# Which engine waits for the last store of a two-tensor interleave: SyncE or GpSimd

## The chip, the cores and the metric

The kernel runs on one core of one Trainium2 chip. The metric is the time of one execution in microseconds on the device, for which the median of several runs is given. The profile is that of one execution; its span goes from the start of the first instruction of the kernel to the end of the last, so the time of the same execution is a little longer than its span.

## The reference

Two tensors x and y of 32 x 256 x 1024 float32 values (33.55 MB each) are interleaved along the last dimension. Nothing is calculated; every value is copied once.

```python
result = np.zeros((batch, seq, dim * 2), dtype=np.float32)
result[..., 0::2] = x
result[..., 1::2] = y
```

## The kernel before

Both inputs are cut into n = 8 pieces of 128 partitions x 8192 values (4 MB each), and piece k of the output is 128 x 16384 values. As each partition takes a contiguous run of the flat tensor, weaving x and y element by element in a partition gives the wanted output.

On chip there are two buffers for x, two for y (128 x 8192 values each, used in turn by k), and two output buffers ot0 and ot1, each of which holds half of an output piece (4 MB). The engines work side by side, each along its own queue, with semaphores between them:

- **SyncE** issues the loads. The first half of the first x piece is issued at L37 (ScalarE issues the other half at L38), and these two are moved by hand ahead of the opening barrier of the program. The loop at L40 issues x (L45) and y (L48) of every piece; from k = 2 on it first waits until VectorE has read the buffer (semaphore `woven`, L43 and L47).
- **VectorE** does the weaving. For each half h of a piece it copies x into the even columns of `ot[h]` (L60) and y into the odd ones (L63). It waits for the loads, and at L59 for the store that last emptied `ot[h]` (semaphore `osem[h]`).
- **ScalarE** issues the stores (L68), one of 4 MB for each half, when `woven` says that both copies are done. Store h adds 16 to `osem[h]` when it has landed.
- **GpSimd** and **TensorE** have no work in the body. GpSimd has four small memsets and its share of the barriers in the opening (L84 and L122 are lines of the set-up around the body).

Every DMA adds 1 to its semaphore from each of the 16 DMA engines. After the last store the semaphores have to be brought back to zero and the stores have to be waited for. ScalarE waits at L72 for the last but one store (`osem[0]` at 16 n = 128) and clears all semaphores but `osem[1]` in one instruction (L75). The very last store counts on `osem[1]`. SyncE waits for it at L76, with a no-operation that starts when `osem[1]` has reached 128 and then takes 128 from it, which brings it to zero. In the profile this instruction is an `EVENT_SEMAPHORE` of the engine's queue. Nothing follows it on SyncE.

Of the kernel before, what the change touches and what calls it, by code (L numbers as in the profile page):

```python
# [3 lines left out]


def _interleave(nc, x, y, out):
    P = 128
    W = 8192
    H = W // 2  # L10

    total = 1
    for s in x.shape:
        total *= s
    n = total // (P * W)
    assert n * P * W == total

    def rows(ap, names, k):
        flat = ap.rearrange("b s d -> (b s d)")
        return flat[k * names : (k + 1) * names].rearrange("(p w) -> p w", p=P)  # L20

    fp32 = mybir.dt.float32
    xt = [nc.alloc_sbuf_tensor(f"xt{b}", [P, W], fp32).ap() for b in (0, 1)]
    yt = [nc.alloc_sbuf_tensor(f"yt{b}", [P, W], fp32).ap() for b in (0, 1)]
    ot = [nc.alloc_sbuf_tensor(f"ot{b}", [P, W], fp32).ap() for b in (0, 1)]

    xsem = [nc.alloc_semaphore(f"xsem{b}") for b in (0, 1)]
    hsem = nc.alloc_semaphore("hsem")
    ysem = [nc.alloc_semaphore(f"ysem{b}") for b in (0, 1)]
    woven = nc.alloc_semaphore("woven")  # L30
    osem = [nc.alloc_semaphore(f"osem{b}") for b in (0, 1)]

    xs = [rows(x, P * W, k) for k in range(n)]
    ys = [rows(y, P * W, k) for k in range(n)]
    os_ = [rows(out, 2 * P * W, k) for k in range(n)]

    nc.sync.dma_start(out=xt[0][:, :H], in_=xs[0][:, :H]).then_inc(xsem[0], 16)  # L37
    nc.scalar.dma_start(out=xt[0][:, H:], in_=xs[0][:, H:]).then_inc(hsem, 16)  # L38

    for k in range(n):  # L40
        b = k % 2
        if k >= 2:
            nc.sync.wait_ge(woven, 4 * (k - 2) + 3)  # L43
        if k:
            nc.sync.dma_start(out=xt[b], in_=xs[k]).then_inc(xsem[b], 16)  # L45
        if k >= 2:
            nc.sync.wait_ge(woven, 4 * (k - 2) + 4)  # L47
        nc.sync.dma_start(out=yt[b], in_=ys[k]).then_inc(ysem[b], 16)  # L48

    for k in range(n):  # L50
        b = k % 2
        for h in (0, 1):
            c = slice(h * H, (h + 1) * H)
            if h == 0:
                nc.vector.wait_ge(xsem[b], 16 * (k // 2 + 1))
            elif k == 0:
                nc.vector.wait_ge(hsem, 16)
            if k:
                nc.vector.wait_ge(osem[h], 16 * k)  # L59
            nc.vector.tensor_copy(out=ot[h][:, 0::2], in_=xt[b][:, c]).then_inc(woven, 1)  # L60
            if h == 0:
                nc.vector.wait_ge(ysem[b], 16 * (k // 2 + 1))
            nc.vector.tensor_copy(out=ot[h][:, 1::2], in_=yt[b][:, c]).then_inc(woven, 1)  # L63

    for k in range(n):
        for h in (0, 1):
            nc.scalar.wait_ge(woven, 4 * k + 2 * h + 2)
            nc.scalar.dma_start(  # L68
                out=os_[k][:, h * W : (h + 1) * W], in_=ot[h]
            ).then_inc(osem[h], 16)  # L70

    nc.scalar.wait_ge(osem[0], 16 * n)  # L72
    used = sorted(s.num for s in [*xsem, hsem, *ysem, woven, osem[0]])
    assert used == list(range(used[0], used[-1] + 1)), used
    nc.scalar.sem_clear(range(used[0], used[-1] + 1))  # L75
    nc.sync.nop(nofuse=True).wait_op(osem[1], 16 * n, "sem-ge").then_inc(  # L76
        osem[1], -16 * n
    )


def kernel(tc, x, y, out):
    nc = tc.nc
    tc.close()
    tc.compile()  # L84

    _interleave(nc, x, y, out)

    blocks = nc.main_func.blocks
    for engine in (mybir.EngineType.SP, mybir.EngineType.Activation):
        opening = blocks[0].instructions  # L90
        at, moved = next(
            (b, i)
            for b in blocks[1:]
            for i in b.instructions
            if i.engine == engine and i.opcode == "DMACopy"
        )
        assert not (moved.sync_info and moved.sync_info.on_wait)
        body = at.instructions
        body.remove(moved)
        gate = next(  # L100
            n
            for n, i in enumerate(opening)
            if i.engine == engine and i.opcode == "Drain"
        )
        opening.insert(gate, moved)
        at.instructions = body
        blocks[0].instructions = opening


# [1 line left out]
_INS = ['x', 'y']  # L111
_OUTS = [((32, 256, 2048), 'float32')]


# [23 lines left out]
```

## Time and profile before

| what | value |
|---|---|
| runs before | 314.41, 314.45, 314.48, 314.58 us; median 314.47 |
| time of the profiled execution | 314.41 us |
| span of the profiled execution | 313.1 us (313.086) |
| instructions | 113 |
| data read and written | 67.11 MB and 67.11 MB, 429 GB/s over the span |
| VectorE busy | 72.6 us (23%), 32 copies |
| GpSimd busy | 0.2 us, 4 memsets, all in the first 0.5 us |
| last copy of VectorE ends | 298.2 us |
| last store issued | 298.24 us |
| ScalarE's clear (L75) starts | 303.40 us |
| SyncE's closing wait (L76) starts | 313.07 us |

In the profile's names, SP is SyncE, ACT is ScalarE, DVE is VectorE, POOL is GpSimd and PE is TensorE; a q behind the name means the queue of the engine, whose instructions (DMA issues, semaphore waits, drains) are not counted as busy time. Where a line gives three durations, these are the least, the median and the greatest in ns, followed by the first and last start in us. In the list of waits a line names who waited, for whom, the total in us, how often, and the longest. The trace also has a record of each update of a semaphore, with its time; those go on a little beyond the span.

### The profile page before, as it was taken

The page shows a single profiled execution, that of the slowest core. Times are in us where ns is not written, and L with a number is a line of the kernel's source. Part 1 is how long each engine was busy: PE and PEld are TensorE (multiplying, and loading weights), DVE is VectorE, ACT ScalarE, POOL GpSimd, SP SyncE. Part 2 cuts the span into 40 slices and gives each one's busy share as a digit, 9 for nine tenths or more (in the row PEclk, how much of TensorE's full clock was granted, in tenths as well). Part 3 has the DMA queues.
Part 4 walks back from the last instruction along what each step waited for, and adds up shares of the span by engine and source line. Part 5 has one row for each costly group of instructions (what it writes and reads, how often), then busy time and mean ns, then how long its engine had stood idle before and what let it go on. Part 6 is the DMA issues. An engine that isn't in the chain of part 4 may idle for free.

```text
span 313.1 us, 113 instructions
## 1 busy us (share of the span) xinstructions
DVE 72.6 (23%) x32; POOL 0.2 (0%) x4
## 2 busy tenths in 40 slices
DVE  0226002231022410324003250031501305013500
POOL 0000000000000000000000000000000000000000
DMA  8999999999999999999999999999999999999998
GB/s 341 463 406 398 465 406 456 414 452 419 435 435 419 452 402 469 402 469 402 465 406 461 410 452 419 435 435 427 444 406 465 402 469 402 465 406 461 410 456 347
DMA packets 4752, 134.22 MB, mean 429 GB/s; under 512 B 528, under 2 KB 528, under 8 KB 528
## 3 DMA queue, kind: packets, MB, share of 16 engines
q10 hardware_dynamic: 2448, 69.21, 51.2%
q1 hardware_dynamic: 2304, 65.01, 48.5%
HBM read 67.11 MB, written 67.11 MB: 429 GB/s over the span
## 4 chain that ended last, share of the span: by engine, by line
DMA 82%; DVE 12%; issue 0%
DMA out_dram<-ot 76%; DMA yt<-in_y_dram 6%; DVE ot L63 6%; DVE ot L60 6%
## 5 line engine op out<-in xcount | busy, mean ns | idle before, releaser
L60 DVE COPY ot<-xt 128x4096 f32<-128x4096 f32 x16 | 36.7, 2295 | 182.8 <-DMA out_dram<-ot 171.3
L63 DVE COPY ot<-yt 128x4096 f32<-128x4096 f32 x16 | 36.7, 2291 | 42.8 <-DMA yt<-in_y_dram 42.8
L122 POOL MEMSET const-bfloat16-1.0<- 128x1 bf16 x1 | 0.1, 102 | 0.0
L122 POOL MEMSET const-uint8-127<- 128x1 uint8 x1 | 0.1, 102 | 0.0
L122 POOL MEMSET const-float32-0.0<- 128x1 f32 x1 | 0.1, 99 | 0.2 <-issue 0.2
L122 POOL MEMSET const-float32-1.0<- 128x1 f32 x1 | 0.1, 99 | 0.0
## 6 DMA issues: line engine op xcount, KB each, us to landing
out_dram<-ot ACTq DMA_DIRECT2D x16, 4096.0 KB, 29.0
yt<-in_y_dram SPq DMA_DIRECT2D x8, 4096.0 KB, 60.8
xt<-in_x_dram SPq DMA_DIRECT2D x7, 4096.0 KB, 43.7
xt<-in_x_dram SPq DMA_DIRECT2D x1, 2048.0 KB, 11.6
xt<-in_x_dram ACTq DMA_DIRECT2D x1, 2048.0 KB, 13.2
```

The lines of the kernel that those rows point to most:

```text
L60: nc.vector.tensor_copy(out=ot[h][:, 0::2], in_=xt[b][:, c]).then_inc(woven, 1)
L63: nc.vector.tensor_copy(out=ot[h][:, 1::2], in_=yt[b][:, c]).then_inc(woven, 1)
L122: nc = _bacc.Bacc("TRN2", target_bir_lowering=False, num_devices=1)
```

## The change

The closing no-operation is issued on GpSimd's queue in place of SyncE's. Its wait (`osem[1]` at 16 n) and its update (minus 16 n) are the same. ScalarE's wait for the last but one store and its clear of the other semaphores stay as they are.

```diff
     nc.scalar.sem_clear(range(used[0], used[-1] + 1))
-    nc.sync.nop(nofuse=True).wait_op(osem[1], 16 * n, "sem-ge").then_inc(
+    nc.gpsimd.nop(nofuse=True).wait_op(osem[1], 16 * n, "sem-ge").then_inc(
         osem[1], -16 * n
     )
```

## Prediction

> **What bounds the kernel.** I read the chain of waits first. Nearly all of it is transfers: 82% of the chain is DMA, mostly stores, and VectorE has 12%. Its last pieces, the DMA issues and the queue waits are the part that the change touches.
>
> ```profile
> DMA 82%; DVE 12%; issue 0%
> ...
> out_dram<-ot ACTq DMA_DIRECT2D x16, 4096.0 KB, 29.0
> ```
>
> ```profile
> 265.56 28.13 DMA out_dram<-ot
> 293.69 0.02 issue
> 293.71 2.30 DVE ot L60
> 296.01 2.20 DVE ot L63
> ```
>
> The last copy ends at 298.21 us. ScalarE issues the last store at 298.24 and its 16 parts land from 312.66 to 313.05. Then only the end is left. For it I read the waits of SyncE's queue and the two closing lines, one by one:
>
> ```profile
> SPq L76 <- SPq L76: 85.9, 1, 85.9
> ```
>
> ```profile
> L76 SPq EVENT_SEMAPHORE  x1: 17/17/17, 313.1 to 313.1; - x1
> ```
>
> ```profile
> L75 ACTq EVENT_SEMAPHORE_RANGE_CLEAR  x1: 63/63/63, 303.4 to 303.4; - x1
> ```
>
> SyncE has sat at L76 since 227.2 us and starts it at 313.069, 16 ns after the last landing. ScalarE was through its own end at 303.467. The span stops when L76 ends (313.086 us), but the time of this execution is 314.41 us, so 1.32 us lie around the span. The semaphore updates of the trace show what comes behind it. Nothing in the kernel uses semaphore 2. It is updated in passes of nine, one pass just before the span, one broken into pieces in it and behind it, one at the very end. In us from the span's start:
>
> ```
> before:  -0.374 -0.340 -0.302 -0.258 -0.234 -0.123 -0.084 -0.050 -0.003
> middle:   1.794 303.585 303.624 303.668 313.220 313.264 313.303 313.337 313.384
> last:   314.170 314.204 314.243 314.286 314.309 314.409 314.447 314.481 314.528
> gaps, before: 34 38 44  24 111 39 34 47 ns (371 in all)
> gaps, middle:  - 39 44   - 44  39 34 47
> gaps, last:   34 39 43  23 100 38 34 47 (358 in all)
> ```
>
> I take this as a walk over the five engines, there and back: four steps out, a turning point, four steps home. The broken middle pass tells who is where. Its second update comes 118 ns after ScalarE's last instruction (303.467), its fifth 134 ns after SyncE's (313.086). So **ScalarE is second and SyncE is the turning point**. The first, at 1.794, belongs to an engine that was done early, which VectorE (busy until 298.2) was not. The length of the steps places the rest. At the barriers that open the kernel, all on one release, the wait instruction of each engine starts this long after the update:
>
> ```
> SyncE 16 ns, ScalarE 21, VectorE 28, TensorE 28 (releases at 0.825, 1.152, 1.480 us)
> GpSimd 24 ns, on its own semaphore (updates at 0.697, 1.025, 1.352 us)
> ```
>
> On the way home the steps are 44, 39, 34 and 47 ns. VectorE, GpSimd, ScalarE, TensorE would give this order (28, 24, 21 and 28, TensorE's instruction being the longest, 51 ns against 17 to 21). So **GpSimd is third and VectorE fourth**; I give that order 8 in 10. [...]
>
> **The change part by part.** One instruction moves from SyncE's queue to GpSimd's. No transfer, copy or semaphore value changes, and nothing else stood behind L76 in either queue.
>
> *Removed from SyncE.* Its 85.9 us of waiting cost nothing: after its last load was issued (226.830 to 227.158) it has nothing to do. It gets to its place in the walk early, but it cannot turn the walk before VectorE has passed it on. Worth 0 by itself.
>
> *Added to GpSimd.* It is idle from 1.5 us to the end, with no instruction of the kernel behind the wait, so nothing is held up inside the kernel. These rows show that the kind of instruction costs as much there as on SyncE:
>
> ```profile
> L84 POOLq EVENT_SEMAPHORE  x4: 17/17/17, 1.0 to 1.5; - x4
> ...
> L84 POOLq DRAIN  x2: 34/38/41, 0.9 to 1.2; - x2
> ...
> L84 SPq EVENT_SEMAPHORE  x2: 17/17/17, 1.2 to 1.5; - x2
> ```
>
> Duration: 17 against 17 ns, 0. Start after the last update: 24 against 16 ns, **+8 ns**. Way from its last instruction to its update of semaphore 2: the trace doesn't show it, as GpSimd was long there when ScalarE handed on. Bounds: ScalarE's 118 ns below, TensorE's 235 ns above if it is the first (1.559 to 1.794), against SyncE's 134: -16 to +101 ns. I take 134, **+0**, because GpSimd's and SyncE's steps elsewhere are alike (two neighbouring instructions 78 to 81 ns apart on GpSimd, 71 to 92 on SyncE). Were a drain in that way, it is 34 to 181 ns more (the longest is this one, with memsets before it):
>
> ```profile
> L122 POOLq DRAIN  x1: 181/181/181, 0.3 to 0.3; - x1
> ```
>
> *Moved: the place at which the walk is stopped.* Before, the late engine is the turning point: VectorE, GpSimd and ScalarE have gone out already (303.668 at the latest), and 44+39+34+47 = 164 ns of way home remain. After, the late one is third: outward to VectorE and SyncE is still to be done, and then home. What that takes is read from the whole passes, from the third update to the ninth: -0.302 to -0.003 = 299 ns, 314.243 to 314.528 = 285 ns. The middle pass had 164, so **+121 to +135 ns**. That is more than two steps (44+24 = 68): in whole passes the fourth engine needs 100 to 111 ns from the turn to its update, and 44 where it had waited long. I read this as its own time between two updates (135 and 123 ns); it would again have just updated. If that reading is wrong the sum is +68.
>
> [...]
>
> *Cover.* Neither ScalarE's end at L75 nor the copies move. SyncE's wait hid beside the transfer, GpSimd's does as well; only what follows the last landing counts, and nothing is beside that. [...]
>
> **Sum.** +8, +0, +128 (the middle of 121 and 135) = +136 ns. The profiled execution's 314.41 us becomes 314.55. The median of the runs is 0.06 above it, so 314.47 + 0.14 = **314.61 us**, +0.04%. Bounds: 8-16+68 = +60 ns below, 8+101+135 = +244 above, and 8+181+135 = +324 with the long drain, +425 with both. One case below that: if the time is not taken at the end of this sequence but where the kernel's last instruction ends, only +8 ns would be seen. Runs differ by 0.17 us among themselves (314.41 to 314.58).
>
> **The rivals.**
>
> *The walk is elsewhere, or isn't timed (no change, not slower).* If the clock that gives the time stops before the walk, the sum is +8 ns, 314.48 us. For it: I cannot see the stop. Against it: 1.32 us lie outside the span, and no transfer of the trace and no kernel instruction fills them. If GpSimd is first and not third, the whole pass counts, 358 to 371 less 164 = +194 to +207, 314.68 us; if fourth, 242 to 270 less 164 or so, +83 to +97, 314.57 us. Both are inside the forecast's own band.
>
> *GpSimd has more to do on its way out (slower, inside 0.2%).* A drain of 34 to 181 ns in its way, hidden so far behind ScalarE's 303.585: +0.17 to +0.32 us, 314.79 us at its long end.
>
> *GpSimd's next instructions are not at hand (slower for certain).* The mechanism on the other side of the bound: after 311 us at one instruction GpSimd has to fetch what follows, at the only place where nothing hides it. Price from this trace: instruction blocks of 8192 B take 0.31 to 0.49 us in transfer (11 to 8 us before the span), and the first transfer of the kernel starts moving 0.985 us after its issue at 0: some 1.3 to 1.5 us. With the walk's +0.14 that is 314.47 + 0.14 + 1.40 = 316.01 us. It passes the 0.2% bound as soon as the way out is 0.49 us longer than SyncE's. Against it: SyncE stood in the same place for 85.9 us and went out in 134 ns, and the trace has no instruction fetch inside the span.
>
> *Faster.* GpSimd would have to beat SyncE's way out by more than the walk's 0.13 us, that is to need no time at all. I see no mechanism for 0.6 us.
>
> **How the numbers follow.** Forecast, +0.06 to +0.25 us: 0.74. Drain or the like on the way out, +0.25 to +0.6: 0.08. Nothing to be seen: 0.08. Fetch or another slow way out, over +0.63: 0.08. Faster by over 0.63 us: 0.02. The bound of 0.2% (0.63 us) is about what a measurement of this kernel can tell from no change; the first three cases lie within it, 0.90. The range goes from the lower edge of the case of no change with the runs' own spread (314.40) to both bounds added (+0.43, 314.90) and 0.10 of spread, 315.00; it leaves out the last two cases.
>
> **What would show it.** L76 appears in GpSimd's queue, starting some 24 ns after the last landing at the same place relative to the last store; the span is the same within 0.1 us. The middle pass of semaphore 2 then has two early updates, at 1.8 and 303.585, and seven late ones: the third some 134 ns after GpSimd's instruction, the fourth and fifth within 70 ns, the ninth some 285 to 299 ns after the third. Three early updates would mean that GpSimd is fourth; none, that it is first. A gap over 0.3 us between L76 and the third update would show a slow way out. The prediction is wrong if the time moves by over 0.43 us with the stores unmoved, or if the stores themselves move.

## The result and the profile after

The changed kernel takes 315.08 us (median of 32 runs, 314.83 to 315.7), the kernel before 314.57 us (52 runs, 314.31 to 315.6): ratio 1.0016 with a 95% interval from 1.0011 to 1.0021, which is +0.50 us (0.35 to 0.66). The forecast was 314.61 us with a range up to 315.0. The profiled execution took 315.00 us against 314.41.

Up to the last landing nothing has moved. The chain of waits of the changed kernel ends with the same four pieces within 0.05 us (start, length, what):

```profile
265.60 28.12 DMA out_dram<-ot
293.72 0.02 issue
293.75 2.30 DVE ot L60
296.04 2.20 DVE ot L63
```

The closing line now stands in GpSimd's queue (least, median and greatest duration in ns, then the first and last start in us), and it is as short there as it was on SyncE, 17 ns:

```profile
L76 POOLq EVENT_SEMAPHORE  x1: 17/17/17, 313.1 to 313.1; - x1
```

And the span, at which most would look first, is that of before to the tenth:

```profile
span 313.1 us, 113 instructions
```

So the half microsecond lies behind the span. The time of a run less its span says the same, without the spread of the stores: 1.27 to 1.38 us in the runs of before that were taken beside the experiments (median 1.31 to 1.33 by set of runs), 1.83 to 1.93 us in 33 of the changed kernel (median 1.88). That is +0.55 us, and the two ranges are far apart. The updates of semaphore 2 show where it is (us from the span's start):

```
after, last landing at 313.083, L76 from 313.106 to 313.123
middle:   1.794 303.607 313.686 313.730 313.753 313.851 313.890 313.924 313.971
last:   314.757 314.791 314.830 314.873 314.896 314.996 315.034 315.068 315.115
```

Two updates are early and the third is the first late one, so GpSimd is third in the walk of the semaphore updates. From the third to the ninth it takes 285 ns, as in the last pass of the kernel before (314.243 to 314.528); from the ninth to the first of the last pass it takes 786 ns, as before too (313.384 to 314.170), so what delays the walk is passed on in full, as the prediction's sum takes it. But between the end of L76 and the third update there are **563 ns**, where SyncE had 134.

### The profile page after: what moved, and what is told of

It is laid out like the page before. It is cut to its first block, busy times and chain, and to the rows that moved or that the text cites. A ratio compares the mean times of both kernels' runs of the same rounds, so it can differ in the third digit from the quotient of the medians.

```text
span 313.1 us, 113 instructions
## 1 busy us (share of the span) xinstructions
DVE 72.6 (23%) x32; POOL 0.2 (0%) x4
## 4 chain that ended last, share of the span: by engine, by line
DMA 82%; DVE 12%; issue 0%
DMA out_dram<-ot 76%; DMA yt<-in_y_dram 7%; DVE ot L63 6%; DVE ot L60 6%
```

## The experiments

The theory after this result, F: GpSimd needs a fixed 0.56 us from its last instruction to its place in the end walk, whenever it gets there. Its main rival, C: the queue was cold after standing still for 311 us. A third, D, looks for a drain of GpSimd in that way. In all that follows "way out" is the time from the end of an engine's last instruction to its update of semaphore 2.

**gp_relay: the way out when nobody waits for it.** SyncE keeps the closing wait; GpSimd stands before ScalarE at the last but one store.

```diff
-    nc.scalar.wait_ge(osem[0], 16 * n)
+    nc.gpsimd.nop(nofuse=True).wait_op(osem[0], 16 * n, "sem-ge").then_inc(hsem, 1)
+    nc.scalar.wait_ge(hsem, 17)
```

> SyncE waits for the last store as before; GpSimd waits for the last but one and hands on to ScalarE through hsem, which then clears. Theory F (fixed): GpSimd always needs some 0.56 us from its last instruction to its update of semaphore 2 (0.563 us in the changed kernel), whenever it gets there and however long it waited. Then its update comes at 303.4 + 0.6 = 304.0 us instead of 39 ns behind ScalarE's, all hidden under the last store, and the time is that of before (0 +/- 0.1 us). Theory L (last): GpSimd is slow only when everybody waits for it, or when nothing else runs; then its update follows ScalarE's (about 303.65) by 39 ns. The time is the same by both; the gap tells them apart.

The lines of GpSimd's wait and SyncE's closing wait in this kernel:

```profile
L72 POOLq EVENT_SEMAPHORE  x1: 17/17/17, 303.6 to 303.6; - x1
```

```profile
L77 SPq EVENT_SEMAPHORE  x1: 17/17/17, 313.3 to 313.3; - x1
```

The middle pass of semaphore 2 (us from the span's start):

```
middle:   1.794 303.867 304.218 304.262 313.447 313.491 313.530 313.564 313.610
```

GpSimd ends at 303.657 us. ScalarE's update comes at 303.867, GpSimd's at 304.218: 351 ns behind it and not 39, and 561 ns behind its own last instruction. SyncE's way out is 134 ns as before, and from its update to the ninth it takes 163 ns against 164. The time is that of before: 314.46 against 314.58 us, ratio 1.0002 (0.9992 to 1.0013), and time less span 1.34 against 1.33 us. So GpSimd's way out is as long when nobody waits for it, 561 against 563 ns, here hidden under the last store, which lands some 9 us later; F holds. By C, too, it could be long here, after 302 us of standing still. One form of C can be read from this trace: a fetch of the instructions behind the kernel. The trace records such transfers ahead of the span (blocks of 8192 B, 0.31 to 0.55 us each), but the last record of an instruction transfer ends at -0.067 us, while the records of the stores go on to 312.943, well past this way out. No recorded fetch fills it.

**gp_warm: the queue kept running.**

```diff
+    for part in (1, 6, 11):
+        nc.gpsimd.wait_ge(osem[1], 16 * (n - 1) + part)
     nc.gpsimd.nop(nofuse=True).wait_op(osem[1], 16 * n, "sem-ge").then_inc(
```

> The changed kernel, with three more waits on GpSimd, for 1, 6 and 11 of the 16 parts of the last store, so that its queue runs until the end and doesn't stand still for 311 us. Theory F (fixed way out): L76's end to the third update of semaphore 2 stays 0.56 us, the time that of the changed kernel, +0.5 us over before. Theory C (cold: GpSimd has to wake up or fetch what follows after the long wait): the gap shrinks towards SyncE's 0.134 us, and the time falls by some 0.4 us to +0.1 us over before.

The four waits were joined into two instructions with two waits each:

```profile
L78 POOLq EVENT_SEMAPHORE  x2: 42/42/43, 313.4 to 313.5; - x2
```

The last ends at 313.547, the third update is at 314.109: 562 ns. Time 315.27 against 314.58 us, ratio 1.0018 (1.0008 to 1.0027); from the last landing to the end of the walk it is 117 ns longer than in the changed kernel, as an instruction was added. But the edit did not keep the queue running as it was meant to: the first of the joined waits starts only at 313.414, 25 ns behind the last landing (313.389). The way out is that of F, but this run says little against C; gp_nops is the test.

**gp_nops: four instructions behind the wait.**

```diff
+    for step in (1, -1, 1, -1):
+        nc.gpsimd.nop(nofuse=True).then_inc(osem[1], step)
```

> The changed kernel with four more no-operations on GpSimd behind L76, which add and take 1 on osem[1]. Theory F: they follow L76 promptly, some 35 to 80 ns apart, and the gap from the last of them to the third update of semaphore 2 is again 0.56 us; the time is the changed kernel's +0.15 to +0.35 us. Theory C (cold): a gap of 0.3 us or more stands between L76 and the first of the four, and the way out behind the last is short, 0.13 to 0.2 us; the time is about the changed kernel's plus the four.

```profile
L80 POOLq EVENT_SEMAPHORE  x4: 17/17/17, 312.9 to 313.2; - x4
```

L76 starts at 312.865, the four at 312.943, 313.021, 313.100 and 313.178: 78 or 79 ns from one to the next, no gap before the first. Behind the last, after 0.3 us of steady work, the way out is 561 ns. Time 315.45 against 314.58 us, ratio 1.0024 (1.0015 to 1.0032); the end is 312 ns later behind the last landing than in the changed kernel, which is four steps of 78. C is refuted: the next instruction of the kernel starts 78 ns after L76's start with no gap before it, and the way out is 561 ns also from a queue that has just run.

**gp_drain and gp_drain2: a drain or two behind the wait.**

```diff
+    nc.gpsimd.drain()
```

> The changed kernel with a drain on GpSimd behind L76. Theory D (the way out is a drain of GpSimd that has to rouse its cores): the kernel's own drain takes 0.2 us or more, and the gap from its end to the third update of semaphore 2 is shorter than 0.56 us by as much. Theory F without a drain as its main part: the drain takes 0.03 to 0.18 us as in the opening, the gap behind it stays 0.56 us, and the time is the changed kernel's +0.08 to +0.25 us.

> The changed kernel with two drains on GpSimd behind L76. With one drain, the way out behind it was 0.524 us in place of 0.561 to 0.563: 37 ns shorter. Theory D (a drain is one step of the way out, and finds nothing left to do when the kernel has just drained): behind the second drain the way out is 0.524 us again, and the second drain itself is shorter than the first one's 34 ns. Theory N (the 37 ns are chance): 0.56 us. Neither explains the other 0.5 us; if a drain was the main part, two would have to take away more than one.

```profile
L79 POOLq DRAIN  x1: 34/34/34, 313.1 to 313.1; - x1
```

```profile
L80 POOLq DRAIN  x1: 34/34/34, 313.1 to 313.1; - x1
```

The first line is of the kernel with one drain, the second is the second drain of the kernel with two. Each takes 34 ns, short as F expected, but the way out behind it does not stay at 0.56 us: it is 524 ns after one and 525 after two. The first drain starts 64 ns after L76 ends, the second 26 ns after the first. So a drain as the first step of the way out would account for the difference: 64 + 34 + 465 = 563 behind a wait, 26 + 34 + 465 = 525 behind a drain. The 465 is what is left over, not measured by itself, and another kind of first step that also starts 38 ns sooner behind a drain would fit these two runs as well. The second drain was not shorter than the first, against that expectation: the saving is in the step to it, not in the drain. From the last landing to the end of the walk it takes 59 ns more than in the changed kernel with one drain, under the 80 that were expected at the least, and 120 ns more with two. Times: 315.06 us, ratio 1.0017 (1.0008 to 1.0026), and 315.20 us, ratio 1.0025 (1.0014 to 1.0036).

**gp_memset: late work on GpSimd.**

```diff
+    scratch = nc.alloc_sbuf_tensor("scratch", [P, 1], fp32).ap()
+    nc.gpsimd.memset(scratch, 0.0)
```

> The changed kernel with a memset of 128x1 on GpSimd behind L76, which gives its cores their last work at the very end instead of at 0.4 us. Theory Q (the way out waits for GpSimd's cores, as the drain of 181 ns behind the opening memsets did): the gap from L76's end to the third update of semaphore 2 grows well beyond the memset's step, to 0.75 us or more (0.56 + 0.1 for the memset + 0.1 to 0.15). Theory S (the way out is a fixed row of the queue's own instructions, 0.427 us more than SyncE's, some five of the 78 ns steps): the gap grows only by the step of one instruction, 0.03 to 0.1 us, to 0.60 to 0.66 us.

```profile
L80 POOL MEMSET scratch<- x1: 98/98/98, 313.1 to 313.1; 128x1 f32 x1
```

From L76's end to the third update it takes 713 ns, 150 more than in the changed kernel, between what the two theories expected. The memset runs from 313.124 to 313.222, the update is at 313.735, 513 ns behind it. Less the 465 ns of above, 48 ns are left between the end of the memset and the end of a drain. In the opening of the kernel before, the drain of 181 ns ends at 0.480 us, 50 ns behind the last of its memsets (0.430). That agrees with a way out that starts with a drain, which ends 48 ns after the memset does, and 465 ns behind it that don't depend on the memset. Time 315.27 us, ratio 1.0021 (1.0009 to 1.0032).

**gp_dma: GpSimd's own DMA queue used.** A small DMA, whose data the kernel does not use, is added at the start.

```diff
+    gsem = nc.alloc_semaphore("gsem")
+    scratch = nc.alloc_sbuf_tensor("scratch", [P, 16], fp32).ap()
+    nc.gpsimd.dma_start(out=scratch, in_=xs[0][:, :16]).then_inc(gsem, 16)
+    nc.gpsimd.wait_ge(gsem, 16)
+    nc.gpsimd.sem_clear(range(gsem.num, gsem.num + 1))
```

> The changed kernel, with one small DMA on GpSimd's queue at the start (64 B of each of 128 rows of x into a scratch buffer, waited for and its semaphore cleared at once), which the kernel doesn't use. So far the way out reads as a drain (64 ns of step and 34 ns) and 0.465 us behind it that no record shows. Theory R (the 0.465 us are spent on GpSimd's own DMA queue, and hang on what it has done): L76's end to the third update of semaphore 2 changes by over 0.05 us from 0.563. Theory S (a fixed row of the queue's own steps): 0.56 us as before. The time is the changed kernel's by S, within the spread of its runs, plus what the small DMA at the start disturbs.

```profile
L82 POOLq EVENT_SEMAPHORE  x1: 17/17/17, 313.2 to 313.2; - x1
```

```profile
q0 software_dynamic: 32, 0.01, 0.0%
```

The first line is the closing wait, the second the additional DMA queue, which neither kernel has without this edit. Way out 562 ns (313.188 to 313.750), time 315.03 against 314.49 us, ratio 1.0016 (1.0005 to 1.0027). That is 1 ns from the changed kernel's 563; S holds.

**dve_waits, pe_waits, act_waits: the other engines.** In the first two the closing no-operation is put on VectorE or TensorE (`nc.vector.nop`, `nc.tensor.nop`). In the third ScalarE waits for both stores:

```diff
     nc.scalar.wait_ge(osem[0], 16 * n)
+    nc.scalar.wait_ge(osem[1], 16 * n)
-    used = sorted(s.num for s in [*xsem, hsem, *ysem, woven, osem[0]])
+    used = sorted(s.num for s in [*xsem, hsem, *ysem, woven, *osem])
-    nc.sync.nop(nofuse=True).wait_op(osem[1], 16 * n, "sem-ge").then_inc(
-        osem[1], -16 * n
-    )
```

> VectorE in place of SyncE has the closing wait. Theory W (each step of the end pass is what the sum of the prediction said, and the long way out belongs to GpSimd alone): VectorE is fourth, so the fourth update is the first late one; wait start after the last landing 28 ns (+12), way out near SyncE's 134 ns, fourth to ninth update 241 ns against 164 (+77): the time is +0.09 us over before, 0.13 with a clock that is a quarter slower. Theory E (every engine but SyncE and ScalarE has a long way out, as they have other units behind them): way out some 0.56 us, +0.5 us as with GpSimd.

> TensorE in place of SyncE has the closing wait. Theory W: TensorE is first; start 28 ns after the last landing (+12), instruction 51 ns (+34), way out 0.13 to 0.235 us (+0 to +101; in the kernel before it was 0.235 from its last barrier instruction), first to ninth update 358 against 164 (+194): the time is +0.24 to +0.34 us over before. Theory E: way out 0.56 us, +0.66 us. If GpSimd and not TensorE were first (it was third in all traces so far), the first update would stay at 1.8 us.

> ScalarE waits for both last stores and clears all eight semaphores, osem[1] too; SyncE has no closing wait. By the walk: start after the last landing 21 ns (+5), the clear 63 ns instead of 17 (+46), way out 118 ns against 134 (-16), second to ninth update 324 against 164 (+160): +0.20 us over before. By theory E, the same. If the place in the walk counts for nothing, +0.04 us.

Their closing lines, VectorE's, TensorE's and ScalarE's (the wait and the clear), one kernel each:

```profile
L76 DVEq EVENT_SEMAPHORE  x1: 21/21/21, 313.0 to 313.0; - x1
```

```profile
L76 PEldq EVENT_SEMAPHORE  x1: 51/51/51, 313.0 to 313.0; - x1
```

```profile
L73 ACTq EVENT_SEMAPHORE  x1: 17/17/17, 313.1 to 313.1; - x1
```

```profile
L76 ACTq EVENT_SEMAPHORE_RANGE_CLEAR  x1: 64/64/64, 313.2 to 313.2; - x1
```

All in one table, from each profiled execution; ns but for the last two columns, which are us. "Start" is from the last landing to the start of the wait, "place" is that of the late engine in the walk, "to the ninth" is from its update to the walk's end.

| kernel, late engine | place | start | way out | to the ninth | landing to ninth | landing to time | time of all runs, ratio |
|---|---|---|---|---|---|---|---|
| before, SyncE | 5 | 16 | 134 | 164 | 331 | 1.357 | 314.57 (with the changed kernel) |
| dve_waits, VectorE | 4 | 29 | 186 | 241 | 477 | 1.507 | 314.66, 1.0007 (0.9995 to 1.0020) |
| act_waits, ScalarE | 2 | 22 | 118 | 324 | 588 | 1.617 | 314.69, 1.0002 (0.9993 to 1.0010) |
| pe_waits, TensorE | 1 | 29 | 278 | 358 | 716 | 1.745 | 314.95, 1.0014 (1.0002 to 1.0026) |
| after, GpSimd | 3 | 23 | 563 | 285 | 888 | 1.917 | 315.08, 1.0016 (1.0011 to 1.0021) |

The first late update is the fourth with VectorE, the second with ScalarE and the first with TensorE, so all five places are as read. Theory E falls: VectorE's way out is 186 ns and TensorE's 278, not 0.56 us. The five ways out are all different here: 118, 134, 186, 278 and 563 ns. VectorE's closing line takes 21 ns against 17; a clock slower by a quarter, which its expectation allows for, was not shown. VectorE's and TensorE's were expected at 134 and at most 235, so from the last landing to the ninth update these kernels take 146 and 385 ns more than the kernel before, against sums of 89 and at most 340. TensorE's is not one constant: in the kernel before it took 235 ns from its last barrier instruction (1.559 to 1.794), and why it is 278 here is not shown. ScalarE's sum was too low by 62 ns (257 against 195), as its second wait was an instruction of its own, 60 ns ahead of the clear. The times of VectorE's and ScalarE's kernels alone would not have told them from no change; the walk does.

**sp_nops: the same four instructions on SyncE.**

```diff
+    for step in (1, -1, 1, -1):
+        nc.sync.nop(nofuse=True).then_inc(osem[1], step)
```

> The kernel before, with four more no-operations on SyncE behind its closing wait, as GpSimd had in gp_nops (78 ns apart there, its way out behind the last one 0.561 us as without them). Theory F: the step is about the same on SyncE, 71 to 92 ns, the way out behind the last is again 134 ns, and the time is +0.28 to +0.37 us over before. If instead something of SyncE's way out can be hidden under instructions of the kernel, the way out is shorter than 134 ns and the time less.

```profile
L80 SPq EVENT_SEMAPHORE  x4: 17/17/17, 313.8 to 314.0; - x4
```

The steps are 57 to 65 ns, shorter than the 71 expected at the least, and the way out behind the last is 132 ns. From the last landing to the ninth update it takes 571 ns, +240 over before, under the 280 expected at the least. The time is 314.70 against 314.56 us, ratio 1.0007 (0.9997 to 1.0018). The four no-operations hide nothing of SyncE's way out, as they hid nothing of GpSimd's.

None of these is measurably faster than the kernel before, and none gave a reason to look for such a version here: SyncE has the fifth and last of the five places, with 164 ns left to the ninth update, and the second shortest way out, 134 ns against ScalarE's 118.

## Why the prediction was wrong

*What bounds the kernel; nothing moves inside it*: right. The stores and the copies start within 0.12 us of before, from 48 us on within 0.05 us, and the span is 313.1 us in both.

*Duration and start of the moved instruction*: right. 17 ns on both, started 23 ns after the last landing against 16, +7 ns (forecast +8).

*The place in the walk*: right. GpSimd third, third to ninth update 285 ns, less 164 = +121 ns (forecast +121 to +135), with 98 ns from the fifth update to the sixth, which the prediction reads as VectorE's turn. The runs show by which update of the pass each engine is held up; whose the last four are is a reading of their gaps and was not shown.

*The way from its last instruction to its update*: **this step failed.** The prediction took "134, +0", with bounds of -16 to +101 ns and 34 to 181 ns more if a drain was in it. It is 563 ns, +429. With it the sum closes: 7 + 0 + 429 + 121 = 557 ns, against 1.917 - 1.357 = 0.560 us from the last landing to the time. (The other 0.03 us between the two profiled executions are the stores, whose last landing was at 313.083 and 313.053.)

The fault was in how the bound was made. GpSimd's way out could not be seen in the trace before, because GpSimd may have been through it at any time between 1.5 and 303.6 us, when ScalarE's update released it. The honest upper bound from that trace was hence not another engine's 235 ns. I took engines as alike because their instructions in the opening step alike (78 to 81 ns against 71 to 92; SyncE's steps there also have one of 58, from 0.912 to 0.970), but no row of the trace shows what the way out is made of, and it differs by engine: 118 to 563 ns. The trace before also has an earlier pass of semaphore 2, from -8.095 to -2.387 us, which the prediction leaves out. Its third update, GpSimd's by place, comes 1.375 us after the second, and the six behind it follow within 301 ns. Why is not shown, but it was a warning: in that pass the late update is the one at GpSimd's place. The rival "GpSimd has more to do on its way out" was right in kind, and the sign named for it, a gap over 0.3 us between L76 and the third update, is the one that came. Its price, from the longest drain of the trace, was too small: 181 ns, where 429 came. A drain at the head of the way out fits the runs (64 + 34 ns), but 465 ns follow it.

*A smaller reading*: if GpSimd were fourth, the whole passes would give 242 and 255 ns, not "242 to 270", so +78 to +91. It does not enter the sum.

*Fetch or a cold queue*: gp_nops, with 561 ns behind four no-operations, refutes the cold queue, and the trace of gp_relay has no record of a fetch in GpSimd's way out (the last one ends at -0.067 us). *The walk isn't timed*: refuted, the time follows the walk within 5 ns in the five kernels of the table (landing to time less landing to ninth: 1.026 to 1.030 us).

**What stays open**: what the 465 ns behind the drain are. The way out they are part of is the same within 2 ns whether GpSimd had stood still for 302 us (gp_relay, 561 ns) or had just run for 0.3 us (gp_nops, 561) and whether its DMA queue was used (gp_dma, 562); if it begins with a drain, the same 465 ns behind that fit with a memset as GpSimd's last work too; no instruction of GpSimd is recorded in them. That the way out begins with a drain is argued from three numbers that agree, not seen.

## What to carry to other kernels

The instruction that was moved here takes 17 ns on either engine; what cost 0.50 us came along with the engine: its way from the last instruction to its update of semaphore 2 (563 ns against 134) and the part of the walk that is left from its place (285 ns against 164). So price these two when an instruction moves at the very end, not the instruction. Read them from the semaphore updates behind the span: the span was 313.1 us in both kernels. Where the trace hides a cost under something longer, do not take other engines' rows as its upper bound: the longest of them was 235 ns here, the cost 563. A kernel that leaves the engine for last among the hidden ones measures it at no cost in time (gp_relay: 561 ns seen, time ratio 1.0002).

## What the runs showed of the hardware

Two things that I had not expected. Each engine had a way out of its own length, and GpSimd's 0.56 us, against 0.12 to 0.28 for the others, is the same within 2 ns in the five kernels in which its last instruction is a wait or a no-operation (561 to 563 ns). And the time that is measured, counted from the span's start, falls on the sixth update of the last pass, which by the prediction's reading is VectorE's way home: 314.409 us for a time of 314.41 in the kernel before, 314.996 for 315.00 in the changed one, 314.640 for 314.64 in gp_relay, 314.716 for 314.72 in pe_waits. In all thirteen profiled executions the two agree within 0.013 us. That the time is taken at this update is not shown, as its start isn't recorded; but what delays the middle pass is in the time in full (1.026 to 1.030 us between its end and the time).
